# Thirty small transfers of a two-block fp32 kernel asked for by ScalarE's queue instead of SyncE's

## The chip, the cores and the metric

The kernel runs on one core of a Trainium2 chip. The metric is the device time of one execution in microseconds; the median of three runs of the kernel before is 1255.97 us. PE is the matrix engine, ACT is ScalarE, DVE is VectorE, POOL is GpSimd and SP is SyncE. SP does no arithmetic here: its queue only asks for transfers (DMAs). ACT can ask for transfers too, from the same instruction stream in which its activations stand.

## The reference, cut to what matters

Input x is 256 tokens by 1024 channels in fp32. A first block mixes with a gated delta rule and a banded attention and ends in a gated MLP; a second block of two layers puts 16 meta tokens ahead (272 rows) and mixes with a gated linear attention and a forgetting attention. The change touches three places of it: the cumulative decays `g` of the delta rule, the triangular solve of the delta rule, and the cumulative forget gates `c` of the forgetting attention.

```python
def chunk_gated_delta_rule(q, k, v, g, beta):        # block 1, 8 heads, chunks of 64
    g = jnp.cumsum(g, axis=-1)
    diff = g[..., :, None] - g[..., None, :]
    decay = jnp.where(causal, jnp.exp(jnp.where(causal, diff, 0.0)), 0.0)
    a_low = jnp.where(strict, jnp.einsum("bnhid,bnhjd->bnhij", k_beta, k) * decay, 0.0)
    rhs = jnp.concatenate([v_beta, k_beta * jnp.exp(g)[..., None]], axis=-1)
    sol = lax.linalg.triangular_solve(a_low + eye, rhs, left_side=True, lower=True, unit_diagonal=True)
    ...                                              # scan over the chunks with u, w = split(sol)

def forgetting_attention(q, k, v, log_f):            # block 2, both layers, 8 heads
    c = jnp.cumsum(log_f.astype(jnp.float32), axis=1)
    logits = jnp.einsum('bqhd,bkhd->bhqk', q_b, kf) + c_b[..., None] - c_k[:, :, None, :]
    logits = jnp.where(key_pos[None, :] <= q_pos[:, None], logits, -jnp.inf)
    return jnp.einsum('bhqk,bkhd->bqhd', jax.nn.softmax(logits, axis=-1), vf)
```

## The kernel before, in words

**Weights.** All weights lie in one array `wall` and are read once, in the order in which they are used, in pieces of mostly 1 MB (`load`, L341) into three buffers `raw`. Each piece holds two tiles of 128x1024. For full fp32 accuracy a tile is split in a high and a low part: ACT copies it to `wh` (four buffers, L313), DVE takes the rest into `wl` (four buffers, L316), and PE multiplies three times (`xh` by `wh`, `xl` by `wh`, `xh` by `wl`, L328): 24 matmuls of 256 or 272 columns per tile. So ACT and DVE must each finish a tile before PE comes to it, and a `raw` buffer is free for SP's next request when both are done with its tiles. L313, L316, L325, L328 and L332 are helpers: nearly every ACT, DVE and PE instruction has one of these lines.

**The places that the change touches.** In `delta_setup` DVE scans the decays into `g`; L827 writes them to a DRAM scratch `gd`. In `decay`, for a pair of heads at a time, L880 reads two rows of `gd` back, repeated over all 128 partitions (its tile is called `k` in the trace). In `delta_rest` L923 writes the diagonal parts of the scores to a scratch `ld` (two transfers), L927 reads the 16x16 diagonal blocks back (`td`), DVE inverts the blocks in 15 steps (L936), L944 writes the inverses and their transposes to `ed0` and `ed1`, and L946 reads both back as full matrices `ee`, which the delta rule's matmuls then use. In block 2, once in each layer, L1419 writes the scanned forget gates to a scratch `cd`, and eight transfers (L1425 and L1426, for four pairs of heads) read them back repeated over 128 partitions as `X2` (272 KB each) and `X1` (144 KB each). ACT meanwhile computes `dec` and `ge` for the linear attention. DVE copies `X0` from `X1` (L1444), POOL masks them (L1446), DVE subtracts scores and takes the maximum (L1503, `fp`), ACT exponentiates, DVE normalises (`fpp`), and PE transposes `fpp` (L332).

**What sets the order.** The program is written as generators, but the order of the instructions on each engine is made by `_Order`: a list scheduler with a table of durations, which goes through time, starts on each engine the ready instruction of highest priority, and then fixes that order. In the kernel before, all transfers are on SP; their model has one chain of 440 ns per request (`ring`) and one of transfer times (`wire`), 1200 ns (`SLACK`) are added to the end of each transfer that isn't a weight or an input, and such a transfer may run at most 24 PE instructions ahead of its place in the program.

**Completion.** A transfer counts up one of eight completion semaphores, named DMAHW0 to DMAHW7 in the listings below, which are handed out in turn over all transfers; a transfer may therefore have to wait until an older one with the same semaphore has landed.

## Time and profile before

| what | value |
|---|---|
| median of three runs | 1255.97 us (1250.74, 1258.10, 1255.97) |
| the profiled execution's own time | 1249.03 us |
| its span, first to last instruction | 1247.3 us |
| mean granted clock of PE | 0.995 |
| busy share: PE, DVE, ACT, POOL | 98%, 82%, 63%, 2% |
| moved by DMA | 232.59 MB, mean 186 GB/s |

The profile is of one execution. A timeline gives an instruction's start and duration; "idle before" is the time for which its engine had nothing to do, with the work that ended it. The chain that ended last goes back from the last instruction over what released each. The duration of a transfer's line on SP is the time that the request took on the queue; when the data is there is told as "to landing". The profiled execution is 6.9 us under the median of the three runs, 0.5%.

### The profile page before, as it was taken

Reading aid. Unit: us, or ns where it says so; the run is one execution under the profiler, and the core shown is the slowest. Engines: PE = TensorE matmul, PEld = TensorE weight load, DVE = VectorE, ACT = ScalarE, POOL = GpSimd, SP = SyncE. Lnnn points to the kernel's source line nnn. Section 1 sums busy time; section 2 is a strip of 40 time slices with the busy share of each in tenths; the row PEclk is TensorE's granted clock in tenths of the full one; section 3 lists DMA queues with packets and bytes.
Section 4 is the critical chain, followed back from the end, with each engine's and each line's share of the span. In section 5 each row is a group of like instructions: output and inputs, shape, how many; then the busy total and the mean of one; then the engine's idle time right before and its main releaser. Section 6 shows DMA issues by size and latency. Waiting matters only on the chain.

```text
span 1247.3 us, 24659 instructions
## 1 busy us (share of the span) xinstructions
PE 1219.5 (98%) x9824; PEld 1166.4 (94%) x9824; DVE 1017.8 (82%) x2098; ACT 781.8 (63%) x1451; POOL 22.2 (2%) x79
## 2 busy tenths in 40 slices
PE   7999999999999899999999999999999999999997
PEld 6898999989999899999877999999999979999996
DVE  6767898789999999767967989996567688999854
ACT  5577855346657768546766776665466576766642
POOL 0000100000000000000020000000001000000000
PEclk9999999999999999999999999999999999999998
DMA  9945577717663576554341444555455326555551
GB/s 360 368 170 188 203 256 234 300 35 265 213 231 137 178 274 220 187 189 169 116 177 69 164 174 171 170 168 183 164 179 192 116 69 203 188 184 181 180 186 47
DMA packets 51123, 232.59 MB, mean 186 GB/s; under 512 B 10536, under 2 KB 19904, under 8 KB 27456
## 3 DMA queue, kind: packets, MB, share of 16 engines
q1 hardware_dynamic: 51008, 231.02, 52.5%
q8 instruction: 77, 1.26, 0.4%
q14 instruction: 38, 0.31, 0.1%
HBM read 226.52 MB, written 4.48 MB: 185 GB/s over the span
## 4 chain that ended last, share of the span: by engine, by line
PE 84%; DVE 7%; DMA 4%; ACT 2%; issue 1%; SPq 0%; DVEq 0%; ACTq 0%
PE acc L328 60%; PE att L328 22%; DMA raw<-wall 3%; PE att L332 3%; DVE wl L316 2%; DVE raw L325 1%; DMA X<-cd 1%; ACT wh L313 1%; DVE res L316 0%; ACT tmp L313 0%; DVE fy L325 0%; DVE fp L1503 0%; DVE xl L316 0%; ACT L313 0%; ACT bq L313 0%
## 5 line engine op out<-in xcount | busy, mean ns | idle before, releaser
L313 ACT ACTIVATE wh<-raw 128x1024 fp32r<-128x1024 f32 (+1 forms) x367 | 381.5, 1042 | 280.8 <-PE acc L328 212.6
L316 DVE TENSOR_TENSOR wl<-raw,wh 128x1024 fp32r<-128x1024 f32 (+1 forms) x367 | 442.2, 1207 | 110.0 <-ACT wh L313 107.5
L328 PE MATMUL acc<-xh,wh 128*128 128x256 f32 (+2 forms) x1312 | 380.2, 291 | 1.4 <-ACT xh L313 0.9
L328 PE MATMUL acc<-xh,wl 128*128 128x256 f32 (+2 forms) x1312 | 374.9, 286 | 0.7 <-DVE wl L316 0.7
L328 PE MATMUL acc<-xl,wh 128*128 128x256 f32 (+2 forms) x1312 | 374.7, 286 | 0.0
L328 PEld LDWEIGHTS acc<-xh,wh 128*128 128x128 f32 x1312 | 246.7, 188 | 6.7 <-issue 2.4
L328 PEld LDWEIGHTS acc<-xh,wl 128*128 128x128 f32 x1312 | 247.4, 189 | 2.9 <-issue 1.4
L328 PEld LDWEIGHTS acc<-xl,wh 128*128 128x128 f32 x1312 | 247.4, 189 | 2.0 <-issue 1.5
L328 PE MATMUL att<-xh,wh 128*128 128x256 f32 (+2 forms) x568 | 161.2, 284 | 1.5 <-ACT wh L313 1.5
L328 PE MATMUL att<-xh,wl 128*128 128x256 f32 (+2 forms) x568 | 161.2, 284 | 0.4 <-DVE wl L316 0.4
L328 PE MATMUL att<-xl,wh 128*128 128x256 f32 (+2 forms) x568 | 161.1, 284 | 0.0
L328 PE MATMUL acc<-ah,wl 128*128 128x256 f32 (+1 forms) x528 | 149.9, 284 | 0.0
L328 PE MATMUL acc<-al,wh 128*128 128x256 f32 (+1 forms) x528 | 149.9, 284 | 0.0
L328 PE MATMUL acc<-ah,wh 128*128 128x256 f32 (+1 forms) x528 | 149.8, 284 | 0.0
L328 PEld LDWEIGHTS att<-xh,wh 128*128 128x128 f32 x568 | 106.8, 188 | 2.4 <-ACT wh L313 2.0
L328 PEld LDWEIGHTS att<-xh,wl 128*128 128x128 f32 x568 | 106.9, 188 | 0.7 <-DVE wl L316 0.6
L328 PEld LDWEIGHTS att<-xl,wh 128*128 128x128 f32 x568 | 106.8, 188 | 0.4
L328 PEld LDWEIGHTS acc<-al,wh 128*128 128x128 f32 x528 | 100.2, 190 | 0.0
L328 PEld LDWEIGHTS acc<-ah,wh 128*128 128x128 f32 x528 | 100.1, 190 | 0.0
L328 PEld LDWEIGHTS acc<-ah,wl 128*128 128x128 f32 x528 | 100.0, 189 | 0.0
L325 DVE SCALAR_TENSOR_TENSOR fy<-fsr,vec,fy 128x256 f32<-128x256 f32 (+2 forms) x176 | 85.6, 489 | 2.1
L325 DVE SCALAR_TENSOR_TENSOR raw<-raw,cact 128x1024 f32<-128x1024 f32 x48 | 58.6, 1221 | 18.3 <-DMA raw<-wall 13.6
(367 smaller groups left out, 1935.9 us busy)
## 6 DMA issues: line engine op xcount, KB each, us to landing
raw<-wall SPq DMA_DIRECT2D x183, 1024.0 KB, 4.9
raw<-wall SPq DMA_DIRECT2D x23, 896.0 KB, 4.5
X<-cd SPq DMA_DIRECT2D x8, 272.0 KB, 5.3
bq<-band SPq DMA_DIRECT2D x8, 256.0 KB, 6.1
ed<-td SPq DMA_DIRECT2D x2, 1024.0 KB, 11.3
X<-cd SPq DMA_DIRECT2D x8, 144.0 KB, 5.1
raw<-wall SPq DMA_DIRECT2D x2, 512.0 KB, 5.3
k<-gd SPq DMA_DIRECT2D x4, 256.0 KB, 5.5
```

What stands on the lines that cost most here:

```text
L313: return self.nc.scalar.activation(out=out, in_=in_, func=func, **k)
L316: self.nc.vector.tensor_tensor(out=out, in0=a, in1=b, op=op)
L325: self.nc.vector.scalar_tensor_tensor(out=out, in0=a, scalar=s, in1=b, op0=op0, op1=op1, **k)
L328: self.nc.tensor.matmul(out, lhsT, rhs, start=start, stop=stop)
L332: self.nc.tensor.transpose(out, in_, self.ident[p0:p0 + n, p0:p0 + n])
```

## The change

`self.small` names the queue of the small transfers. It was SP's and is now ACT's; L827, L880, L1419, L1425 and L1426, which named SP's queue directly, take `self.small` as well, and the four places of `delta_rest` (L923, L927, L944, L946) took it already, so they move with it. These are 12 transfers in block 1 and 9 in each layer of block 2, 30 in all. The rest of the diff is in the scheduler: the moved transfers keep their costs of the SP table, but have a chain `side` of their own beside the weights', get 600 ns added to their end instead of the 100 ns and the `SLACK`, take 400 ns of ACT's time each, and the rule of 24 PE instructions no longer holds for them.

```diff
--- before.py
+++ after.py
@@ -260,7 +260,7 @@
         for idx, n in self.chunks:
             self.coff.append(o)
             o += n * P
-        self.small = self.nc.sync
+        self.small = self.nc.scalar
         self.raw, self.hl, self.pre = {}, {}, {}
         self.loaded = self.split = 0
         self.cur = 0
@@ -824,7 +824,7 @@
         self.ts(e, e, nega)
         nc.vector.tensor_tensor_scan(out=g, data0=self.c("rst", 0, S, 32, 40), data1=e, initial=0.0, op0=MUL, op1=ADD)
         gd = self.pd.tile([8, S], F32, tag="gd", name="gd")
-        nc.sync.dma_start(out=gd, in_=g)
+        self.small.dma_start(out=gd, in_=g)
         self.gd = gd
         G = [g[:, 64 * c + 63:64 * c + 64] for c in range(4)]
         br = self.t(pa, (40, 6, P), "ee")[R]
@@ -877,7 +877,7 @@
         b0 = self.bT[:, 0:32].rearrange("p (c h) -> p h c", h=8)[:, h:h + 2, :]
         b1 = self.bT[:, 32:48].rearrange("p (c h) -> p h c", h=8)[:, h:h + 2, :]
         grow = self.t(pa, (P, 2, S), "k2", 4)
-        nc.sync.dma_start(out=grow, in_=self.gd[h:h + 2].rearrange("h s -> (h s)").unsqueeze(0).to_broadcast([P, 2 * S]))
+        self.small.dma_start(out=grow, in_=self.gd[h:h + 2].rearrange("h s -> (h s)").unsqueeze(0).to_broadcast([P, 2 * S]))
         M = self.BQ[:, h:h + 2, 1, :]
         M0, M1 = M[:, :, 0:S], M[:, :, S:384]
         for j in range(2):
@@ -1416,14 +1416,14 @@
         nc.vector.tensor_tensor_scan(out=c, data0=self.c("ones", 0, 1, 32, 40).to_broadcast([8, L]), data1=E[R, 2, :],
                                      initial=0.0, op0=MUL, op1=ADD)
         cd = self.pd.tile([8, L], F32, tag=f"cd{i}", name=f"cd{i}")
-        nc.sync.dma_start(out=cd, in_=c)
+        self.small.dma_start(out=cd, in_=c)
         X2 = self.t(pa, (P, 8, L), "X2")
         X1 = self.t(pa, (P, 8, 144), "X1")
         X0 = self.t(pa, (NM, 8, NM), "X0")
         for m in range(4):
             h = slice(2 * m, 2 * m + 2)
-            nc.sync.dma_start(out=X2[:, h], in_=cd[h].rearrange("h s -> (h s)").unsqueeze(0).to_broadcast([P, 2 * L]))
-            nc.sync.dma_start(out=X1[:, h], in_=cd[h, 0:144].unsqueeze(0).to_broadcast([P, 2, 144]))
+            self.small.dma_start(out=X2[:, h], in_=cd[h].rearrange("h s -> (h s)").unsqueeze(0).to_broadcast([P, 2 * L]))
+            self.small.dma_start(out=X1[:, h], in_=cd[h, 0:144].unsqueeze(0).to_broadcast([P, 2, 144]))
         yield
 
         self.dec = dec = self.t(pa, (P, 2, 5), "dec")
@@ -1709,7 +1709,7 @@
             if i.is_transpose:
                 return max(2 * n, m) / 2.4 + 2
             return 4 * max(n, min(m, 128)) / 2.4 + (4 if int(ins[1].ap[0][1]) == 128 else 100)
-        if e == "SP":
+        if kind == "InstDMACopy":
             o = outs[0]
             rows = int(o.ap[0][1])
             dims = [(int(s), int(c)) for s, c in o.ap]
@@ -1829,7 +1829,8 @@
         for k in range(n):
             left[k] += len(self.deps[k])
             for j, after in self.deps[k].items():
-                succ[j].append((k, self.WAIT[eng[j]][E.index(eng[k])] if after or eng[j] != eng[k] else 0))
+                q = "SP" if self.ins[j].name in self.fix else eng[j]
+                succ[j].append((k, self.WAIT[q][E.index(eng[k])] if after or q != eng[k] else 0))
 
         prev = {}
 
@@ -1890,7 +1891,7 @@
                 heapq.heappush(soon[eng[k]], (0.0, k))
         for key in self.rows:
             give(key)
-        wire, ring, table, done = 0.0, 0.0, 0, 0
+        wire, side, ring, table, done = 0.0, 0.0, 0.0, 0, 0
         order = {e: [] for e in E}
         array = [0.0] * 8
         port = 0.0
@@ -1932,6 +1933,10 @@
                 if self.ins[k].name not in self.free:
 
                     end[k] += self.SLACK
+            elif self.ins[k].name in self.fix:
+
+                side = max(side, s + 440 + self.fix[self.ins[k].name]) + self.dur[k]
+                end[k], clock[e] = side + 600, s + 400
             elif len(self.cols.get(k, range(8))) < 8:
 
                 at = max([ready[k]] + [array[c] for c in self.cols[k]]) + self.dur[k]
```

The scheduler works out a new order for all engines; up to about 97 us of the run before it is the same. Three places of it matter below. In the listings names carry the buffers' numbers, and `waits` lists the semaphores that an instruction waits for.

**ACT at the end of the triangular solve (block 1).** The four requests `ed` (write the inverses) and `ee` (read them back) stand on SP before, among the weights:

```order
L341 DMA raw_459_2868<-wall 128x2048 [waits DMAHW3_49,DMAHW0_49,DVE_49]
L944 DMA ed_1069<-k_322_1974 128x16x16 [waits DVE_49,Pool_49]
L944 DMA ed_1070<-k_322_1974 128x16x16 [waits DVE_49]
L341 DMA raw_463_2901<-wall 128x2048 [waits DMAHW1_49,DVE_49]
L946 DMA ee_2099<-ed_1069 128x16x128 [waits DMAHW4_49]
L341 DMA raw_478_2987<-wall 128x2048 [waits DMAHW2_49,DVE_49]
L946 DMA ee_2099<-ed_1070 128x16x128 [waits DMAHW5_49]
L341 DMA raw_485_3029<-wall 128x2048 [waits DMAHW3_49,DVE_49]
```

and after the change on ACT, among the splits of the weight tiles:

```order
L944 DMA ed_1069<-k_322_1974 128x16x16 [waits DVE_49]
L313 ACTIVATE tmp_435_2712<-tmp_433_2705 128x256 [waits DVE_49,Activation_49]
L944 DMA ed_1070<-k_322_1974 128x16x16 [waits DVE_49]
L313 ACTIVATE wh_454_2832<-raw_443_2758 128x1024 [waits PE_49]
L313 ACTIVATE wh_460_2870<-raw_447_2791 128x1024 [waits DMAHW2_49,PE_49]
L946 DMA ee_2099<-ed_1069 128x16x128 [waits DMAHW4_49]
L313 ACTIVATE vb_1173<-acc_446_2789 128x256 [waits PE_49]
L313 ACTIVATE tmp_450_2821<-vb_1173,vec_67 128x256 [waits Activation_49]
L946 DMA ee_2099<-ed_1070 128x16x128 [waits DMAHW5_49]
L313 ACTIVATE wh_464_2903<-raw_459_2868 128x1024 [waits DMAHW3_49,PE_49]
L313 ACTIVATE tmp_456_2860<-acc_453_2831,hb_1635 128x256 [waits PE_49]
```

The second `ee` is ahead of the split `wh_464`, and waits for the landing of the second `ed` (DMAHW5) before anything behind it can start. On PE the first matmul that reads `ee` stood in row 1,532 of its order and now stands in row 1,487, 45 rows of single dense matmuls earlier.

**ACT at the gates of layer 0 (block 2).** Before, SP had `cd` and the eight `X` in one run, with the next weights behind:

```order
L341 DMA raw_1314_7997<-wall 128x2048 [waits DMAHW6_49,DVE_49,Activation_49]
L1419 DMA cd_7536<-gy_7511 8x272 [waits DVE_49,Pool_49]
L1425 DMA X_1228_7538<-cd_7536 128x544 [waits DMAHW2_49]
L1426 DMA X_1229_7539<-cd_7536 128x2x144
...
L1426 DMA X_1229_7539<-cd_7536 128x2x144
L341 DMA raw_1331_8089<-wall 128x2048 [waits DMAHW3_49,DVE_49]
L341 DMA raw_1354_8199<-wall 128x2048 [waits DMAHW4_49,DVE_49]
```

Now ACT has them, `cd` ahead of a table load and the first `X` behind the `dec` and `ge` activations:

```order
L313 ACTIVATE wh_1315_7999<-raw_1296_7896 128x1024 [waits DMAHW0_49,PE_49]
L1419 DMA cd_7536<-gy_7511 8x272 [waits DVE_49]
L313 ACT_TABLE_LOAD
L313 ACTIVATE dec_7551<-gy_7511 128x4 [waits DVE_49]
L313 ACTIVATE ge_7512<-ge_7512 128x272 [waits DVE_49]
L313 ACTIVATE dec_7551<-gy_7511 128x4
L313 ACTIVATE ge_7512<-ge_7512 128x272 [waits DVE_49]
L1425 DMA X_1228_7538<-cd_7536 128x544 [waits DMAHW2_49]
L1426 DMA X_1229_7539<-cd_7536 128x2x144
...
L1426 DMA X_1229_7539<-cd_7536 128x2x144 [waits DMAHW3_49]
L313 ACTIVATE wh_1323_8042<-raw_1296_7896 128x1024 [waits PE_49]
L313 ACTIVATE wh_1332_8091<-raw_1314_7997 128x1024 [waits PE_49]
```

What stood on ACT directly behind the last `ge`, the split `wh_1323`, now stands behind all eight requests. On PE the first transpose of `fpp` stands four dense matmuls later in the weight tile it interrupts (after 20 of the tile's 24 instead of 16). In layer 1 the order on ACT has the same form: `cd`, table load, `dec`, `ge`, `dec`, `ge`, eight `X`, then the split; there the first transpose of `fpp` stands 8 dense matmuls earlier than before.

## Rows read from the trace of the kernel before

**Rows 1.** The page: busy time, share of the span and instructions of each engine, and the chain that ended last, by engine and by line.

```profile
PE 1219.5 (98%) x9824; PEld 1166.4 (94%) x9824; DVE 1017.8 (82%) x2098; ACT 781.8 (63%) x1451; POOL 22.2 (2%) x79
...
PE 84%; DVE 7%; DMA 4%; ACT 2%; issue 1%; SPq 0%; DVEq 0%; ACTq 0%
PE acc L328 60%; PE att L328 22%; DMA raw<-wall 3%; PE att L332 3%; DVE wl L316 2%; DVE raw L325 1%; DMA X<-cd 1%; ACT wh L313 1%; DVE res L316 0%; ACT tmp L313 0%; DVE fy L325 0%; DVE fp L1503 0%; DVE xl L316 0%; ACT L313 0%; ACT bq L313 0%
```

**Rows 2.** Stretches of the core. Columns: from:to and length in us, then busy us (instructions) of PE, PEld, DVE, ACT and POOL, the granted clock, the DMA engines' busy share, GB/s.

```profile
110.00:125.00 15.00, 14.85 (x101) 12.33 (x100) 14.06 (x58) 10.87 (x37) 0.00 (x0) 1.00 0.20 72
180.00:205.00 25.00, 25.00 (x213) 25.00 (x212) 23.85 (x56) 13.56 (x20) 0.00 (x0) 1.00 0.68 254
...
240.00:250.00 10.00, 9.31 (x103) 7.82 (x101) 8.53 (x19) 2.97 (x7) 0.00 (x0) 1.00 0.57 215
590.00:615.00 25.00, 23.73 (x156) 20.54 (x156) 23.42 (x61) 20.91 (x34) 0.55 (x6) 0.93 0.36 127
...
626.00:633.00 7.00, 5.84 (x47) 5.62 (x45) 5.14 (x24) 3.45 (x13) 5.03 (x12) 1.00 0.92 340
```

**Rows 3.** SP's queue at the end of the triangular solve. Two requests of weights from the timeline (start us, us, engine, line, operation, out<-in, count), then the lines L944 (`ed`) and L946 (`ee`): duration of a request in ns, shortest, median and longest, first and last start, and the time to landing.

```profile
211.86 1.91 SPq L341 DMA_DIRECT2D raw<-wall  x1
...
214.85 4.24 SPq L341 DMA_DIRECT2D raw<-wall  x1
...
L944 SPq DMA_DIRECT2D ed<-k x2: 377/2057/3737, 207.4 to 208.0; - x2
...
DMA to landing us min/median/max: 6.3/6.9/7.5
...
L946 SPq DMA_DIRECT2D ee<-ed x2: 691/738/785, 214.0 to 219.3; - x2
...
DMA to landing us min/median/max: 7.9/8.5/9.1
```

**Rows 4.** ACT over time in the same stretch; in brackets the idle time before the instruction and what ended it.

```profile
211.00 0.36 ACT L313 ACTIVATE vb<-acc 128x256 f32<-128x256 f32 x1
211.40 0.51 ACT L313 ACTIVATE tmp<-vb,vec 128x256 f32<-128x256 f32 x1
212.89 1.06 ACT L313 ACTIVATE wh<-raw 128x1024 fp32r<-128x1024 f32 x1 [0.98 <-PE acc L328]
```

**Rows 5.** The chain that ended last in 200 to 260 us (start us, us, what).

```profile
199.90 30.56 PE acc L328 x257
230.46 1.80 PE att L328 x16
```

**Rows 6.** SP's queue over time from 618 us on (`cd`, first and last `X` of layer 0), and two links of the chain that ended last there.

```profile
618.40 0.29 SPq L1419 DMA_DIRECT2D cd<-gy  x1
619.72 0.34 SPq L1425 DMA_DIRECT2D X<-cd  x1
...
623.38 0.43 SPq L1426 DMA_DIRECT2D X<-cd  x1
...
618.40 1.30 DMA cd<-gy
...
623.38 8.60 DMA X<-cd
```

**Rows 7.** ACT over time in the same stretch.

```profile
617.72 1.06 ACT L313 ACTIVATE wh<-raw 128x1024 fp32r<-128x1024 f32 x1 [0.57 <-PE acc L328]
618.80 1.28 ACT L313 ACT_TABLE_LOAD   x1
...
620.67 0.43 ACT L313 ACTIVATE ge<-ge 128x272 f32<-128x272 f32 x1
621.00 1.05 ACT L313 ACTIVATE wh<-raw 128x1024 fp32r<-128x1024 f32 x1
623.73 1.06 ACT L313 ACTIVATE wh<-raw 128x1024 fp32r<-128x1024 f32 x1 [1.68 <-PE acc L328]
```

**Rows 8.** DVE and PE over time from 631.5 us on.

```profile
632.01 0.17 DVE L1444 COPY X<-X 16x32 f32<-16x32 f32 x1 [1.86 <-DMA X<-cd]
...
631.55 0.29 PE L328 MATMUL acc<-xh,wh 128*128 128x272 f32 x1
633.11 0.63 PE L332 MATMUL att<-ident,fpp 128*128 128x128 f32 x3 [1.27 <-DVE fpp L320]
...
636.46 0.44 PE L332 MATMUL att<-ident,tl 128*128 128x128 f32 x2 [0.93 <-ACT ftA L313]
```

**Rows 9.** Layer 1, the same place: SP (last `X`), ACT and PE over time, and the time to landing of the `X1` transfers (line L1426, both layers).

```profile
941.41 0.50 SPq L1426 DMA_DIRECT2D X<-cd  x1
...
934.98 1.28 ACT L313 ACT_TABLE_LOAD   x1
937.30 0.21 ACT L313 ACTIVATE dec<-gy 128x4 f32<-128x4 f32 x1 [1.03 <-DVE gy L1433]
...
938.85 0.43 ACT L313 ACTIVATE ge<-ge 128x272 f32<-128x272 f32 x1
...
949.48 0.59 PE L332 MATMUL att<-ident,fpp 128*128 128x128 f32 x3
...
DMA to landing us min/median/max: 4.3/5.1/5.8
```

**Rows 10.** The line L880, the four transfers of decay rows: duration of a request in ns, shortest, median and longest, first and last start.

```profile
L880 SPq DMA_DIRECT2D k<-gd x4: 350/392/417, 137.3 to 143.7; - x4
```

## The prediction, made before the changed kernel was run

> **What bounds the kernel now.** I read the page first: PE is busy 98% of the span, 27.8 of 1247.3 us are left, and of the chain that ended last PE has 84%, DMA 4%, of which weights (`raw`) 3% and the read-back of the gates (`X<-cd`) 1% [rows 1]. So a faster transfer only pays where PE stands still for it. The table of stretches shows how little that is behind the start: 180 to 205 us runs 213 matmuls in 25 us without a gap, 0.1174 us each, and a 24-matmul tile takes 2.82 us [rows 2]. PE's stops are few: 0.69 us in 240 to 250 us, 1.16 us in 626 to 633 us, and a thin stretch at 590 to 615 us with 156 matmuls where 213 would fit, where no moved transfer stands [rows 2].
>
> Then I went to the three places of the change. The `ed` and `ee` transfers of block 1 end a chain that PE reaches at 230.46 us straight after 30.56 us of weights [rows 5]: it doesn't wait for them. In layer 0 PE does wait: the chain goes from `cd` over the last `X` (issued at 623.38, 8.60 us long) [rows 6] to DVE's copy at 632.01, which had waited 1.86 us for it, and to the transpose of `fpp` at 633.11, for which PE had stood idle; another 0.93 us of idle time stands before 636.46 [rows 8]. In layer 1 the transpose at 949.48 has no idle time noted before it [rows 9]. So the moved transfers cost PE some 1.4 us in layer 0 and nothing elsewhere. That, not the queues' business, is what can be won directly.
>
> **What the change costs, part by part.** Numbers are differences against the profiled execution (1249.03 us with 1247.3 us of span); I add them to the median of the runs, 1255.97 us, which lies 6.9 us above. A measurement of this kernel tells about 0.5%, 6.3 us, from no change.
>
> *Decay rows (gd, four grow).* ACT gets five requests of 0.35 to 0.42 us [rows 10], 2 us in all, and the first read-back waits on ACT until `gd` has landed; the nearest price for that is `cd`, 1.30 us [rows 6]. Queued behind it are ACT's bias and exponential activations. In 110 to 125 us ACT is busy 10.87 of 15 us and PE 14.85 of 15 [rows 2], so 4 us of room stand against at most 3.4. I take 0; bounds 0 and +1.3. SP loses five requests and weights could be asked for earlier, which is worth nothing while PE runs at 99%.
>
> *Diagonal blocks (ld, td, ed, ee).* Here ACT runs behind a wait. It issues `ed0` at about 207.4 and `ed1` at 208.0. On SP one of these two took 3.74 us, as did weight requests beside them, 1.91 and 4.24 us [rows 3]: the queue did not take them faster. `ee0` then waits for the landing of `ed0`, 6.3 us after 207.4, so 213.7, and takes 0.79; `vb` and `tmp` follow with 0.36 and 0.51 us [rows 4]; `ee1` waits for `ed1`, 208.0 + 7.5 = 215.5, issues at 215.7 and takes 0.69 by the rows of `ee`, or 4.24 by the slow weight beside it. Behind it is the split `wh_464`. Before, that split ran at 212.89, as soon as PE released its buffer [rows 4]; with four buffers three tiles stand ahead of it, 8.5 us, so PE needs it at 221.3. Now it runs at 216.4 to 219.9 and is finished, with 1.06 us, at 217.5 to 221.0: covered, barely in the worst case; without that cover each us of ACT is one of PE. The second thing queued is `ee` itself. PE's order takes its first matmul 45 dense matmuls earlier, 5.3 us, at 225.2 instead of 230.46. `ee1` issued at 215.7 lands after 7.9 to 9.1 us [rows 3], 223.6 to 224.8: in time. With the slow issue it is 229.0, and PE stands 3.8 us, with 0.9 more for DVE's half of the late split. I take 0 from the nearest rows (`ee`'s own); bounds −0.7 (the stop at 240 to 250 us goes, since SP asks for weights without `ed` and `ee` between them) and +4.7.
>
> *Gates of layer 0 (cd, eight X).* Before, SP issued `cd` at 618.40, the eight `X` from 619.72 to 623.81, 4.1 us in all [rows 6]. On ACT `cd` stands behind a split that ends at 618.78, and the eight behind the table load (1.28 us), two `dec` and two `ge`, which ended at 621.10 before [rows 7] and end about 621.4 with 0.29 us of `cd` ahead. So the `X` go out from 621.4 to 625.5, 1.7 us later, the last one starting at 625.1. The split behind them moves from 621.00 to 625.5; PE began that tile 16 matmuls before the transpose, about 629.7, and the split and DVE's `wl` take 2.3 us: covered. When the last `X` lands is open. If it takes 8.60 us again [rows 6] that is 633.7. If it has a weight of 1 MB more ahead, since SP is now free to ask for it 1.7 us sooner, add 2.8 us, 1.05 MB at 340 / 0.92 = 370 GB/s, the rate of the stretch from 626 us scaled to busy engines [rows 2]: 636.5. If it takes the median of these transfers, 5.1 us [rows 9], it is 630.2. From the landing to PE's transpose were 1.1 us (632.01 to 633.11). Without a stop PE would have come to the transpose at 631.67 (the matmul at 631.55 and one step), and comes 4 matmuls, 0.5 us, later by the new order: 632.17. So the stop is 633.7 + 1.1 − 632.2 = 2.6 us instead of 1.44. I take +1.2, by the landing of the same transfer; bounds −1.4 (630.2, no stop) and +4.0 (636.5).
>
> Here a rule speaks the other way. The Trainium skill (DMA: Bandwidth & Descriptors, section Queues, rings and completion order) says that SP and ACT each have rings of their own on the same 16 DMA engines, which take turns between them packet by packet. By that, `X` would not stand behind weights asked for earlier but share with them from its first request. By that rule `X` (1.66 MB) and as much of weights would take 9.0 us at 370 GB/s and, with the 1.3 us of `cd` as a start-up, be through at about 631.7; the stop would shrink to 0.6 us, and this term would be −0.8 instead of +1.2 (an estimate). No row of before shows two queues at work at once, so I keep 8.60 us for the sum.
>
> *Gates of layer 1.* The table load that ran at 934.98 in ACT's idle time before `dec` (1.03 us idle behind it) now stands behind `cd`, which waits for the scan at 936.6. `cd` to 936.9, table load to 938.2, `dec` and `ge` to 939.3, as late as before (938.85 + 0.43). The eight `X` go out from 939.3 on, the last starting at 942.8 instead of 941.41, 1.4 us later [rows 9]. Landing 5.8 us later (longest of the `X1`) is 948.6, and 1.1 us more to the transpose is 949.7. PE comes to it at 949.48 − 8 × 0.12 = 948.5: a stop of 1.2 us. Bounds: 4.6 us to landing hide it (0), 8.60 us give +4.0. I take +1.2.
>
> The sum is 0 + 0 + 1.2 + 1.2 = **+2.4 us, 1258.4 us**; the bounds add up to −2.1 and +14.0.
>
> **Rivals.** *ACT is held by its own requests (slower).* Issues on SP took 1.9 to 4.2 us where weights streamed [rows 3], against 0.3 to 0.5 in the quiet stretch before the `X` [rows 6]. If ACT's queue is held likewise, ACT stands with the splits behind it. It decides from about 3 us in one request: `ee1` then lands behind PE's earlier place (+3.8 to +4.7), and an `X` held for 2 us is late by 2 us more in both layers (+1.2 + 2 each). That is 4.2 + 3.2 + 3.2 = +10.6 us, 1266.6 us. For it: ACT now asks while SP asks too. Against: by rows 6 eight requests in a row were taken at 0.5 us each.
>
> *The queue helps (faster).* The moved transfers overtake weights, SP asks for weights earlier, and the named stops go: 1.4 in layer 0, 0.9 behind it, 0.7 at 240 to 250, −3.0 us, 1253.0 us. To go beyond 0.5% the new order must also fill part of the thin stretch at 590 to 615 us, where 57 matmuls, 6.7 us, are missing: −7, 1249 us. The rule of the Trainium skill above is on its side. Against: PE hardly waits for any of these transfers.
>
> *Hidden anyway (no change).* Both `X` land as early as before in the span that matters, 1256 us.
>
> **How the numbers follow.** The forecast of +2.4 us has a chance of 0.45, ACT held 0.27, the queue helps 0.18, hidden 0.10. Of the faster case I put two thirds, 0.12, beyond 0.5%, because there the whole order moves and the runs shown already differ by 7 us; of the slower case 0.24, and 0.02 of the forecast's upper bound, together 0.26. What is left, 0.62, is within 0.5%. The range goes from 1249.5 us (queue helps) to 1268 us (ACT held, and a little less than the upper bounds together).
>
> **What would show it.** Right: `X` issued on ACT about 621.4 to 625.5 with 0.3 to 0.8 us each, the last landing at 633 to 634, PE idle 2 to 3 us before the transpose of `fpp` in layer 0 and about 1 us in layer 1; `ee` landed before PE's first use. Wrong: requests of 2 us and more on ACT; idle time on PE before the first `ee` matmul or with ACT's `wh` as releaser near 220 us; `X` landing within 5 us of the request, so that the stop of layer 0 is gone; or a thin stretch at 590 to 615 us that has changed its number of matmuls.

## The result, and the profile after

The changed kernel takes 1270.89 us in the median of 4 executions (1263.97 to 1274.66), before 1257.03; the ratio is 1.0117 with a 95% interval of 1.0082 to 1.0152. In another 6 executions the ratio is 1.0130 (1.0080 to 1.0180). It is slower by about 15 us; the range ended at 1268.0. One execution each of ld_td_only (6628 us), of gd_only (2508 us) and of the kernel before (1269.5 us) lies far above the others of its kernel and is left out everywhere below.

The profiled execution took 1268.23 us, with a span of 1266.5 us (before 1247.3). The chain that ended last by engine, a line as in [rows 1]:

```profile
PE 77%; DVE 10%; DMA 6%; ACT 4%; issue 2%; ACTq 1%; POOL 0%; DVEq 0%; POOLq 0%; SPq 0%
```

PE has lost 7 points of the chain to DVE, DMA and ACT. Stretches of the changed kernel, columns as in [rows 2]:

```profile
180.00:185.00 5.00, 5.00 (x44) 5.00 (x43) 3.96 (x7) 2.30 (x3) 0.00 (x0) 1.00 1.01 332
185.00:190.00 5.00, 1.53 (x13) 1.32 (x12) 3.15 (x8) 1.96 (x4) 0.00 (x0) 0.99 0.45 170
190.00:195.00 5.00, 5.00 (x32) 5.00 (x31) 3.76 (x14) 1.42 (x2) 0.00 (x0) 0.67 0.75 259
230.00:235.00 5.00, 3.98 (x33) 3.64 (x32) 2.81 (x4) 0.23 (x2) 0.00 (x0) 1.00 1.04 424
235.00:240.00 5.00, 2.24 (x11) 2.17 (x11) 3.71 (x6) 1.19 (x2) 0.00 (x0) 0.77 0.77 318
640.00:645.00 5.00, 2.98 (x24) 2.75 (x22) 2.94 (x17) 2.62 (x13) 2.64 (x5) 1.00 0.82 278
645.00:650.00 5.00, 3.85 (x21) 3.01 (x21) 5.00 (x11) 2.85 (x5) 1.37 (x6) 0.73 0.33 107
...
690.00:695.00 5.00, 5.00 (x23) 3.44 (x25) 4.16 (x15) 1.55 (x6) 0.00 (x0) 0.50 0.01 3
695.00:700.00 5.00, 5.00 (x34) 3.52 (x32) 1.64 (x3) 1.81 (x5) 0.00 (x0) 0.50 0.00 0
```

At full pace there are 44 or 45 matmuls in 5 us of block 1 and 42 in block 2. PE stands still for 3.5 us at 185; in the 5 us behind it the granted clock, a mean over the stretch of its two levels 1.2 and 2.4 GHz, is 0.67. It stands for 1.0 and 2.8 us at 230 to 240, again with a lower clock behind it, and for 2.0 and 1.2 us at 640 to 650. At 690 to 700 it is busy all the time at a clock of 0.50, 1.2 GHz, with 57 matmuls in 10 us.

To see where the time goes, I compared both traces at equal amounts of PE work (the sum of the usual steps of all matmuls so far). The changed kernel is behind by 1.1 us at 180 us of the time of before, by 6.2 at 190, by 13.7 at 240, by 10.6 from 320 to 630 (it makes up about 3 us between 260 and 320), by 12.8 at 650, by 18.6 from 700 to 940 and by 19.2 at the end. So block 1's solve costs 9.5 us net, layer 0's gates 2.2, a stretch of low clock 5.8, layer 1's gates 0.6. In layer 0 the order on PE differs, so that the 2.2 and the 5.8 are parted only to about 1 us.

**The first stop.** The requests of `ld` and `td`, on SP before, and then ACT around them in the changed kernel, columns as in [rows 4]:

```profile
167.24 0.43 SPq L923 DMA_DIRECT2D ld<-bq  x1
...
174.45 0.38 SPq L927 DMA_DIRECT2D td<-ld  x1
```

```profile
170.59 0.48 ACT L313 ACTIVATE tmp<-acc,hb 128x256 f32<-128x256 f32 x1 [0.84 <-PE acc L328]
170.65 0.38 ACTq L923 DMA_DIRECT2D ld<-bq  x1
...
178.08 1.06 ACT L313 ACTIVATE wh<-raw 128x1024 fp32r<-128x1024 f32 x1 [1.05 <-DMA raw<-wall]
178.15 0.37 ACTq L927 DMA_DIRECT2D td<-ld  x1
```

The second `ld` stands behind an activation that waited for PE until 170.59 (in the kernel before SP asked for it at 167.24); its data had landed by 175.4, but `td` stands behind a split that waited for a weight until 178.08. It was asked for 3.7 us later than before (174.45), 2.8 us later when what the core was behind by then is taken off. DVE before, and in the changed kernel:

```profile
183.95 0.15 DVE L316 TENSOR_TENSOR td<-k,td 128x1 f32<-128x1 f32 x1
```

```profile
184.13 0.48 DVE L325 SCALAR_TENSOR_TENSOR tmp<-vb,vec,tmp 128x253 f32<-128x253 f32 x1
186.85 0.16 DVE L316 TENSOR_TENSOR td<-k,td 128x1 f32<-128x1 f32 x1 [2.23 <-DMA td<-ld]
```

`td` landed 8.7 us after the request (5.8 before). DVE waits 2.23 us for it, and the `tmp` that PE needs next is behind it on DVE (188.52); before, that `tmp` (179.35) stood ahead of it. PE's longest sums of waits, by what ended them (us in all, times, longest):

```profile
PE att L332 <- DVE fpp L320: 3.7, 3, 3.2
PE att L332 <- DVE tmp L325: 3.5, 1, 3.5
PE att L328 <- DVE k L316: 2.8, 1, 2.8
...
PE att L328 <- DMA ee<-ed: 1.0, 1, 1.0
...
PE acc L328 <- ACT wh L313: 0.5, 1, 0.5
```

The 3.5 us for `tmp` are the stop at 185; the 1.0 and the 2.8 are the stops at 230 to 240, the first for `ee`, the second for `k`; of 3.7 us for `fpp` 3.2 are in layer 0. For splits (`wh`) it waited 0.5 us directly, as before.

**The second stop**, ACT's requests with the time to landing of `ee` under them (to be held against [rows 3]):

```profile
212.89 3.90 ACTq L944 DMA_DIRECT2D ed<-k  x1
...
218.73 0.86 ACTq L946 DMA_DIRECT2D ee<-ed  x1
...
220.72 3.63 ACTq L946 DMA_DIRECT2D ee<-ed  x1
```

```profile
DMA to landing us min/median/max: 10.8/11.1/11.5
```

The second `ed` held ACT 3.90 us and the second `ee` 3.63. Both `ee` needed 10.8 to 11.5 us to land instead of 7.9 to 9.1, and the last landed at 232.3, 45 matmuls before its old place in PE's order: PE waited 1.0 us for it. The longer wait behind it, 2.8 us, was not for `ee`. The chain that ended last goes on from the held ACT:

```profile
224.46 1.07 ACT wh L313
...
228.25 1.15 DVE wl L316
...
229.42 5.33 DMA raw<-wall
...
234.85 1.07 ACT wh L313
...
235.95 1.23 DVE wl L316
237.17 0.61 DVE k L316
...
237.83 2.08 PE att L328 x8
```

The split behind the second `ee` was late, with it the low part `wl` on DVE, and so the buffer of that weight came free late (229.4); the next weight landed at 234.75, its split and its `wl` came behind it, and on DVE the `k` that PE waited for stood behind that `wl`. Before, two `k` stood ahead of the `wl`:

```profile
231.38 0.69 DVE L316 TENSOR_TENSOR k<-att,cst 128x512 f32<-128x512 f32 x1 [3.65 <-PE att L328]
...
232.89 1.22 DVE L316 TENSOR_TENSOR wl<-raw,wh 128x1024 fp32r<-128x1024 f32 x1
```

**Layer 0**: ACT's requests, the link of the chain that ended last, and DVE (compare [rows 6] and [rows 8]):

```profile
628.99 0.30 ACTq L1419 DMA_DIRECT2D cd<-gy  x1
...
631.31 0.37 ACTq L1425 DMA_DIRECT2D X<-cd  x1
...
636.12 0.48 ACTq L1426 DMA_DIRECT2D X<-cd  x1
```

```profile
632.71 9.33 DMA X<-cd
```

```profile
642.06 0.17 DVE L1444 COPY X<-X 16x32 f32<-16x32 f32 x1 [2.66 <-DMA X<-cd]
...
644.88 1.36 DVE L320 TENSOR_SCALAR fpp<-fp,den 128x272 f32<-128x272 f32 x3
```

Eight requests took 5.3 us. A weight was asked for on SP at 632.77, amid them; the `X1` issued at 632.71, the fourth request, took 9.33 us. In layer 1, where the next weight was asked for only at 963.9, after the last `X` (961.0), no `X` needed more than 5.7 us.

### The profile page after: what moved, and what is told of

Same layout as the page of the kernel before. It is cut to its first block, busy times and chain, and to the rows that moved or that the text cites. A ratio compares the mean times of both kernels' runs of the same rounds, so it can differ in the third digit from the quotient of the medians.

```text
span 1266.5 us, 24657 instructions
## 1 busy us (share of the span) xinstructions
PE 1229.9 (97%) x9824; PEld 1173.8 (93%) x9824; DVE 1019.4 (80%) x2098; ACT 783.8 (62%) x1453; POOL 24.6 (2%) x79
## 4 chain that ended last, share of the span: by engine, by line
PE 77%; DVE 10%; DMA 6%; ACT 4%; issue 2%; ACTq 1%; POOL 0%; DVEq 0%; POOLq 0%; SPq 0%
PE acc L328 52%; PE att L328 22%; DMA raw<-wall 3%; DVE wl L316 3%; PE att L332 3%; ACT wh L313 1%; DVE raw L325 1%; ACT L313 1%; DMA X<-cd 1%; DMA td<-ld 1%; DVE tmp L325 1%; DMA ed<-k 1%; DVE res L316 0%; ACT tmp L313 0%; DVE fp L1503 0%
## 5 line engine op out<-in xcount | busy, mean ns | idle before, releaser
L325 DVE SCALAR_TENSOR_TENSOR raw<-raw,cact 128x1024 f32<-128x1024 f32 x48 | 58.7, 1223 | 12.7 <-DMA raw<-wall 8.1
## 6 DMA issues: line engine op xcount, KB each, us to landing
ed<-td SPq DMA_DIRECT2D x2, 1024.0 KB, 11.5
```

The lines of the kernel that those rows point to most:

```text
L325: self.nc.vector.scalar_tensor_tensor(out=out, in0=a, scalar=s, in1=b, op0=op0, op1=op1, **k)
```

## The experiments

All ratios are to before's executions on the same chip (medians 1254.0 to 1256.1). They stand with their intervals as recorded and are not the quotients of the medians beside them; in runs of 4 executions the two differ by up to 0.4%.

| run | median us (executions) | ratio (95% interval) |
|---|---|---|
| b1_only | 1265.8 (10) | 1.0096 (1.0066 to 1.0126) |
| b2_only | 1257.5 (10) | 1.0007 (0.9975 to 1.0038) |
| ld_td_only | 1264.2 (9) | 1.0053 (1.0016 to 1.0089) |
| ed_ee_only | 1258.4 (10) | 1.0012 (0.9983 to 1.0042) |
| gd_only | 1256.4 (9) | 1.0015 (0.9990 to 1.0039) |
| ld_old_plan | 1253.4 (10) | 0.9990 (0.9959 to 1.0022) |
| ee_old_plan | 1254.2 (10) | 1.0000 (0.9967 to 1.0033) |
| delta_old_plan | 1254.3 (10) | 1.0001 (0.9969 to 1.0033) |
| sp_optplan | 1262.8 (10) | 1.0082 (1.0044 to 1.0121) |
| mixed_plan | 1263.0 (10) | 1.0075 (1.0043 to 1.0108) |
| b2_old_plan | 1274.5 (4) | 1.0106 (1.0023 to 1.0190) |
| pool_queue | 1274.7 (4) | 1.0184 (1.0121 to 1.0247) |
| plan_wire | 1278.4 (4) | 1.0195 (1.0139 to 1.0251) |
| plan_slack | 1286.7 (4) | 1.0295 (1.0227 to 1.0364) |

**Which transfers.** Parts of the change alone; the others name SP's queue again, as here for `ed` and `ee`:

```diff
-            q.dma_start(out=EE[:, w]...
+            nc.sync.dma_start(out=EE[:, w]...
```

> Only block 1's 12 transfers on ACT, cd and X back on SP. Theory (the late `td` and the held ACT in the triangular solve cost the time, the rest is the clock in block 2): PE stops near 185 us (about 3.5 us) and near 231 to 237 us (about 4 us) as in the changed kernel, net +9 us against before, 1266 us. Rival (block 2's X transfers cost most): 0 to +2 us. Rival (the clock at 50% around 690 us comes from the new order of block 2): if the order of block 2 is again that of before, the clock stays at 1.0 there.

> Only block 2's 18 transfers (cd, X) on ACT. Theory: one stop of 2 to 3.5 us before the transpose of fpp in layer 0 instead of 1.44, +1 to +2 us; and +7 us more (1264 to 1266 us) if PE's thin stretch about 55 us later again lets the clock fall to 0.5, which would show that this is the price of block 2's new order. Rival (the X transfers themselves cost the time by contention): the stop is 5 us and more in both layers.

> Only ld and td (three transfers, L923 and L927) on ACT. Theory: td is again requested 3 to 4 us later than before and lands 8 to 9 us after the request, DVE waits for it and PE stops about 3.5 us near 185 us; +4 to +6 us. `ee`, on SP, is asked for late by what the solve is late, and its place on PE is early, so a stop near 228 us is possible. Rival (only the held ACT at ed and ee costs): 0.

> Only ed and ee (four transfers, L944 and L946) on ACT. Theory: no stop near 185 us; ACT is held 3.9 us by the second ed and 3.6 us by the second ee, ee lands 11 us after its request instead of 8 to 9, PE stops at its first and second ee matmul, together 0 to 4 us since the solve is 5 us earlier than in the changed kernel. Rival (late td is the whole cause, the second stop only its echo): 0.

> Only gd and the four decay rows on ACT, with the new model. By the difference of b1_only (+10.6 us in the medians, +6.0 without the clock's part) and the two halves of the solve (+4.3 and +0.9 without the clock's part) it costs 0 to 2 us. If these five requests are what the two halves leave over in the medians, up to +4 us.

Block 1 carries nearly all, and in it `ld` and `td` the most. b1_only has stops of 3.2, 2.6 and 3.9 us for the same readers, ld_td_only one of 3.2 us at 184 us with DVE waiting 3.5 us for `td`, ed_ee_only 1.4 us for `ee` and 3.3 for `k`, part of which it gets back later. The expectation for gd_only and the order of the parts held. b2_only had the longer stop in layer 0 (4.2 us) but no measurable loss, and not the +7 us for the clock that its expectation allowed for.

**Queue or plan.** The change does two things: it puts transfers on another queue, and it lets the scheduler believe that they run on a lane of their own. These runs keep the queue and give the scheduler most of the old belief back, for `ed` and `ee`, for `ld` and `td`, and for all seven of the solve: the chain shared with the weights and the 1200 ns, though not the rule of 24 PE instructions and not the place in the chain of SP's requests.

```diff
-                side = max(side, s + 440 + self.fix[self.ins[k].name]) + self.dur[k]
-                end[k], clock[e] = side + 600, s + 400
+                wire = max(wire, s + 440 + self.fix[self.ins[k].name]) + self.dur[k]
+                end[k], clock[e] = wire + 100 + self.SLACK, s + 400
```

> Only ed and ee on ACT, and the scheduler models them on the weights' chain with the 1200 ns as before: the first ee matmul is back in row 1,532, PE's order differs from before in 10 lines. If the stop at ee (5 us in ed_ee_only) came from PE's place for ee, 45 matmuls early, there is none now, and the time is that of before within 2 us. If it came from the queue (ACT held, ee landing late), a stop of 3 us and more stays near 230 us.

> Only ld and td on ACT, with the old model for them. If the stop near 184 us comes from the plan, it is gone and the time is within 2 us of before. If it comes from the transfers themselves (the second ld and td land later because they share the DMA engines with the weights instead of standing ahead of them), td still lands 2 to 4 us later than before (180.2) and the stop is smaller, 0 to 2 us, by what the plan allows for.

> All seven transfers of the solve (ld, td, ed, ee) on ACT with the old model for them. PE's order differs from before in 129 lines. If the plan is the cause in block 1, the time is that of before within 3 us (the parts alone gave 0.999 and 1.000). If late td and late ee together are too much even for the old plan, +3 to +6 us.

No loss in any. Stretches of delta_old_plan (5.8 us behind before since 120 us, by a low clock there):

```profile
185.00:195.00 10.00, 10.00 (x86) 10.00 (x86) 9.68 (x24) 5.48 (x8) 0.00 (x0) 1.00 1.01 331
...
230.00:240.00 10.00, 10.00 (x88) 10.00 (x87) 2.87 (x4) 3.61 (x5) 0.00 (x0) 1.00 0.67 282
```

PE does not stop. What differs is told by `td`, in us, each run's times less what it was behind the kernel before at that place (good to some tenths):

| run | `td` asked for | landed | DVE comes to its first reader | DVE waits |
|---|---|---|---|---|
| before | 174.5 | 180.2 | 184.0 | 0 |
| changed kernel | 177.3 | 185.9 | 183.7 | 2.2 |
| ld_td_only | 175.5 | 182.5 | 179.0 | 3.5 |
| ld_old_plan | 177.5 | 183.0 | 183.9 | 0 |
| delta_old_plan | 176.7 | 183.0 | 183.9 | 0 |

The clean pair is ld_td_only and ld_old_plan: the same transfers on the same queue land within 0.5 us of each other, the reader stands 5 us earlier in one, and only there PE stops. DVE in ld_td_only and then in ld_old_plan:

```profile
184.12 0.16 DVE L316 TENSOR_TENSOR td<-k,td 128x1 f32<-128x1 f32 x1 [3.52 <-DMA td<-ld]
```

```profile
183.97 0.16 DVE L316 TENSOR_TENSOR td<-k,td 128x1 f32<-128x1 f32 x1
```

So it is for `ee`: in delta_old_plan the last one landed 4.0 us earlier against PE's work than in the kernel before, in ee_old_plan 0.4 us later, and in the changed kernel some 2 us earlier, where PE came to it 5 us earlier. In the changed kernel `td` is another matter. DVE comes to it when it did before, but it lands 5.7 us later: 2.8 by the later request, which is ACT's order, and 2.9 because it took longer to land. No run parts that longer landing from the order. What the runs show, then, is that ACT's queue alone, with these seven transfers on it, costs nothing in the solve, and that the order made under the new belief brings the stops, by the places of the requests as well as those of the readers.

A kernel with all transfers on SP and a more hopeful plan loses too:

```diff
-    SLACK = 1200
+    SLACK = 500
-            w = 24 if eng[k] == "SP" else None
+            w = None
```

> The kernel before, all transfers on SP, but with the optimistic plan: 500 ns instead of 1200 added, and no rule of 24 PE instructions. If the loss were the plan's optimism alone and not the queue, this loses too: +3 to +9 us. If it is ACT's queue: within 2 us of before.

It loses 8.1 us by the medians and 10 by the ratio, as this belief was expected to, or a little more. But it is not the belief of the change: the transfers still share the weights' chain, and the rule of 24 is dropped for all of SP's transfers. Most of the loss arises at 19 us, far from the solve, where PE waits 10.0 us in one piece for a weight asked for behind a request (L560) that held SP for 8.30 us and that the change does not move; near 250 and 320 us it loses some 3 and 2 us more. It says little on the solve.

**The old belief is no cure for the whole.** plan_wire has the diff with `wire` above for all 30 transfers, plan_slack only `side + 600 + self.SLACK`, b2_old_plan the diff with `wire` for block 2's transfers alone, mixed_plan the old belief for block 1's 12 and the new one for the rest (`B2` holds the names of block 2's):

```diff
+            elif self.ins[k].name in self.fix and self.ins[k].name not in B2:
+                ...
             elif self.ins[k].name in self.fix:
```

> The changed kernel with 1200 ns added again to the end of each moved transfer in the scheduler's model. Theory (the plan puts users of the transfers too early): the stops at td, ee and X shrink by about 1 us each, -2 to -5 us against the changed kernel, 1266 to 1269 us. Rival (the requests come late because ACT is in order, whatever the plan says): as the changed kernel, 1271 us.

> The changed kernel, but the scheduler's model lets the moved transfers and the weights share one chain of transfer times, as before, with the 1200 ns: the first ee matmul then stands 45 places later than before instead of 45 earlier. Theory: the stops at ee are gone (-4 us and its clock loss, -3), that at td partly; 1258 to 1264 us. Rival (requests late by ACT's order): stop at td as in the changed kernel, 1264 to 1271 us.

> Only block 2's cd and X on ACT with the old model for them. plan_wire lost 2% although the solve's halves lose nothing with the old model; the loss of its profile began at 640 us of the time of before, +3.3 at the X of layer 0, +6 at 680 and +10.6 at 690 us. If that is block 2's order, this loses 8 us and more; if it needs block 1's changes too, it is within 3 us of before.

> All 30 transfers on ACT as in the change; the old model (one chain with the weights, 1200 ns) for block 1's 12, the new one for block 2's 18. If the plan for block 1 is what the change pays for, the time is that of before or up to 4 us above (b2_only 1.0007, delta_old_plan 1.0001), against +15 us of the change. If ACT's queue itself costs, it stays at +8 us and more.

All lose. b2_old_plan is the first of its two cases; plan_slack and plan_wire missed; mixed_plan came out at the +9 us of its second case, that ACT's queue itself costs. In block 1 the stop at 185 us is gone in plan_wire and mixed_plan, but with the decay rows on ACT as well the last `ee` lands 15.4 and 15.6 us after its request, and some 6 to 7 us are lost between 230 and 300 us. In mixed_plan the chain that ended last runs through that landing itself: with these 12 transfers in this order the queue is not neutral, and what was found above holds for the seven alone. In block 2 the old belief itself does harm. ACT in b2_old_plan:

```profile
635.99 1.18 ACTq L1426 DMA_DIRECT2D X<-cd  x1
645.44 0.33 ACTq L1425 DMA_DIRECT2D X<-cd  x1
...
646.84 2.95 ACT L313 ACTIVATE wh<-raw 128x1024 fp32r<-128x1024 f32 x3 [11.84 <-DMA raw<-wall]
```

The seventh `X` was issued 8.3 us after the sixth ended, at the moment (645.42) at which the weight asked for at 635.0 landed, with whose completion semaphore it shares its own; three splits stood behind it, ahead of which ACT had computed nothing for 11.84 us, and PE stopped for 3.9 us.

**Another queue without anything behind it.** POOL is 2% busy:

```diff
-        self.small = self.nc.scalar
+        self.small = self.nc.gpsimd
```

> The 30 transfers on POOL's queue, which is 2% busy, instead of ACT's. If ACT's order (requests behind splits, splits behind requests) is the cause, the stops near 185 and 231 us go and the time is that of before or up to 3 us less. If two queues sharing the DMA engines are the cause (td and ee landing 3 us later than before), the stops stay: +4 to +10 us. POOL's own requests may take longer than ACT's; no run here shows that yet.

`td` was asked for at 172.64, right when `ld` had landed, and was there at 179.6. PE's largest waits:

```profile
PE att L332 <- DVE fpp L320: 10.2, 3, 6.3
PE att L328 <- DMA ee<-ed: 3.6, 1, 3.6
```

With +1.84% it lies outside both cases of its expectation. The stop at 185 us is gone, so there it was ACT's order that made `td` late for its reader. The others stay or grow: `ee` had been put 61 rows earlier and took 11.2 to 12.0 us to land, and the `X` of layer 0 landed up to 11.4 us after the request with two weights asked for amid them, a stop of 6.3 us.

**Two queues by themselves.** Transfers without the kernel. In the first try the sections ran into each other and tell nothing of sharing; the second orders them. The core of it:

```python
for name, q, wgt in (("sx", nc.sync, True), ("ax", nc.scalar, True), ("nx", nc.scalar, False), ...):
    for m in range(4):
        q.dma_start(out=big[:, h], in_=...)      # as X2
        q.dma_start(out=one[:, h], in_=...)      # as X1
    if wgt: nc.sync.dma_start(out=w, in_=...)    # 1 MB
```

> Not the kernel: only transfers. Twice over: eight X transfers with a weight of 1 MB behind them on SP (sx); the same with the X on ACT and the weight on SP asked for about 1 us later (ax); the X on ACT alone (nx); one ee-like transfer (2048 pieces of 512 B) with a weight behind it on SP (se), the same on two queues (ae), alone on ACT (ne). Theory (each DMA engine takes turns between the queues, and a turn of weights moves more bytes): in ax and ae the weight lands before or with the small transfer, and the last X and ee land 2 to 5 us later than alone; in sx and se the small transfers land as if alone, and the weight after them. Rival (a queue of its own puts small transfers ahead): ax and ae land like nx and ne.

> Only transfers again, now one section strictly after the other: sx, ax, nx, se, ae, ne twice over (X or ee-like on SP with a weight behind it, on ACT with the weight on SP about 1 us later, on ACT alone). Theory (shared DMA engines, turns between the queues): ae's transfer lands 2 to 5 us later than ne's and than se's, and its weight not later than itself; ax's last X lands 2 to 3 us later than nx's. Rival: ae like ne, ax like nx.

Time to landing of the `X1`-like transfers, alone on ACT, then on ACT with a weight on SP, then on SP with the weight behind them:

```profile
DMA to landing us min/median/max: 3.3/5.1/6.5
...
DMA to landing us min/median/max: 3.6/7.6/7.9
...
DMA to landing us min/median/max: 3.4/4.9/7.8
```

With a weight on the other queue the median of the `X1` is 7.6 us instead of 5.1; on one queue ahead of it they keep 4.9. The weight, asked for amid them, landed with the fourth. The rival is out for `X`. But a reader waits for the last of the eight, and that gains little by one queue: it landed 12.1 and 12.2 us after the first request with the weight on the other queue, 11.3 and 11.9 ahead of it on one, 9.4 and 10.7 alone. The `ee`-like transfer landed after 5.8 to 6.0 us alone, 6.1 to 7.1 with the weight on the other queue, 6.2 ahead of it on one: one weight a microsecond later doesn't explain the 10.4 to 12.7 us of `ee` on ACT in the kernels with the new belief (7.9 to 8.6 in delta_old_plan). What this does not rule out is the spacing: each `ee` is 1 MB like a weight. In the changed kernel the two were asked for 2.0 us apart with two weights just ahead of the second, 4 MB in all, for which the 424 GB/s of the row at 230 would need 9.9 us, by an estimate from that row; before, the two `ee` were 5.3 us apart. No run varies it.

**The spread.**

> The changed kernel again, in more executions, for the spread of the granted clock. If the time without the clock's part is the same in all executions and only the clock differs, then time and mean clock lie on one line as in the executions of before, and the changed kernel loses about 8 us in stops and 4 to 8 us by the clock.

The medians 1270.5 and 1270.9 agree. With the clock's part reckoned as span times what the mean clock lacks to 1, these 6 executions lie some 5 us above before without it (1248.1 to 1243.4), the first 4 some 8 (1251.9), and the rest of the 15 us is the clock. In its profile the solve costs 8.9 us, as in the first one, but the first stop only some 2 of it.

## Why the prediction was wrong

*What bounds the kernel.* Right: PE, and no gain was there to be had. No run was faster than before beyond its interval.

*Decay rows, 0 (to +1.3).* Profile +0.3 us; gd_only 1.0015 with no change inside the interval. Right within what can be told of them alone; in mixed_plan they stand with a loss that the seven others do not have by themselves.

*Diagonal blocks, 0 (−0.7 to +4.7).* **This step failed**: 9.5 us net in the profile, 8.9 in that of changed_again, 1.0096 in b1_only. First, I priced `ed` and `ee` and left `ld` and `td` without a price, though they stand in the same chain and ACT's order shows what they stand behind; with it `td` landed 5.7 us later, DVE, in order, waited 2.23 us for it, and PE lost 5.1 us (some 2 in changed_again). Second, I called the late split covered. It was, for its own tile; but it kept a weight's buffer, the next weight came late, and a `k` that PE needs stood behind that weight's `wl`: 2.8 us. Third, I took `ee`'s landing (7.9 to 9.1 us) from rows in which one queue kept the weights behind it, and it was 10.8 to 11.5, and I read PE's place for `ee`, 45 matmuls early, as a place that the transfer would just reach: 1.0 us. Behind all three is the order made under the scheduler's new belief: with the old one the same seven transfers on the same queue cost nothing (delta_old_plan, 1.0001). With the decay rows on ACT too they do cost under the old belief (mixed_plan, 1.0075); that part stays open.

*The clock* had no term. After each stop the granted clock was lower for a while: at 190 to 195 us PE was busy throughout and ran 32 matmuls instead of 45, some 1.5 us of the first 5.1; at 235 to 240 it was 0.77.

*Layer 0, +1.2 (−1.4 to +4.0).* The size was right: a stop predicted at 2.6 us was 3.2, and PE fell behind by 2.2 us (6.4 in changed_again with the low clock behind the stop). The `X` left between 631.3 and 636.6, which is 620.7 to 626.0 without the 10.6 us that the core was behind; predicted 621.4 to 625.5. The way to it is in part luck. The landing that decided was that of the fourth request after 9.33 us, 2.3 us earlier than the one predicted for the last, and from it to PE's transpose it took 4.1 us, not 1.1, since DVE had a weight's `wl` in between.

*The rule weighed there* would have made this −0.8. That queues take turns, as the Trainium skill has it (DMA: Bandwidth & Descriptors, section Queues, rings and completion order), agrees with two_queues_2, where the weight on the other queue brought the median of the `X1` from 5.1 to 7.6 us. My estimate from it had the wrong sign: the small transfers do not gain by the turns, the weight does, which would have stood behind them on one queue. The Trainium skill's sentence that asking from several engines only saves the time of asking (same page, section Issuing engines are not separate DMA queues) agrees with delta_old_plan, which gained nothing (1.0001, 0.9969 to 1.0033).

*Layer 1, +1.2 (0 to +4.0).* 0.6 us: the last `X` landed 5.4 us after its request.

*Rivals.* "ACT is held by its own requests" named the sign, +10.6 us and the condition, 3 us in one request, which was met twice (3.90, 3.63). Its mechanism does not make the first stop, the larger one; it makes the second by a longer way than the rival had, the late buffer instead of PE's wait for a split. "The queue helps" is refuted for every part. The chance of 0.26 for slower was too low, since it counted one of three things that could fail in the same chain.

**Open** is which interaction makes the solve late when the decay rows are on ACT with the old belief too (mixed_plan against delta_old_plan), and why `td` needs 8.7 us and `ee` 11 in the kernel; for the 5.8 us at 690 us see the last section.

## What to carry to other kernels

A transfer moved to a compute engine's queue stands behind everything that this engine waits for (`td` was asked for 2.8 us later here): go through every link of the chain, and ask of each what is in front of it and who, in order, stands behind its reader. Ask the same of the work behind the request: a split that came late by a request of 3.6 us kept a buffer, and PE stopped 2.8 us for what came of that. When a scheduler gets a new cost for a transfer, price the readers' new places before the transfers: with `td` landing as in ld_old_plan, a reader 5 us earlier gave ld_td_only a stop of 3.2 us. A queue of its own didn't put small transfers ahead of a large one here (7.6 us against 5.1 alone); one queue with the small ones first kept most of them there (4.9), but not the last.

## What the runs showed of the hardware

One kernel spreads by 16 us, and nearly all of it goes with the clock. 31 executions of the kernel before took 1248.45 to 1264.79 us, with mean granted clocks from 0.997 to 0.984; the correlation is −0.93. PE's order in b2_only is that of before up to 595 us. Before from 110 to 120 us, and then b2_only from 110 to 125:

```profile
110.00:115.00 5.00, 4.85 (x28) 3.56 (x27) 4.09 (x18) 2.08 (x5) 0.00 (x0) 1.00 0.15 26
115.00:120.00 5.00, 5.00 (x37) 4.19 (x36) 4.96 (x21) 4.51 (x13) 0.00 (x0) 1.00 0.46 188
```

```profile
110.00:115.00 5.00, 4.85 (x23) 3.53 (x22) 4.13 (x17) 2.08 (x5) 0.00 (x0) 0.84 0.19 34
115.00:120.00 5.00, 5.00 (x21) 3.66 (x21) 2.45 (x8) 2.73 (x6) 0.00 (x0) 0.50 0.43 180
120.00:125.00 5.00, 5.00 (x21) 4.37 (x20) 5.00 (x25) 2.77 (x13) 0.00 (x0) 0.50 0.00 0
```

The first 5 us have the same busy time on PE, 4.85 us, with waits between thin matmuls; in one execution the clock stayed at 2.4 GHz, in the other it fell to 1.2 within them and stayed there for over 10 us, 5.3 us lost. So a low clock that one profile shows behind thin work is not the change's by that alone. The changed kernel's 5.8 us at 690 us are such a case: in the profile of changed_again the clock is 1.00 there, and low at 110 to 125 (5.7 us) and behind the stop of layer 0 (0.50 at 655). PE's order from 640 to 720 us is the same in b2_only as in the changed kernel, and there too the clock at 690 is 1.00; b1_only has the order of before in that stretch, in which the clock before was 1.00, and fell to 0.50 at 690. What is the change's: 10 executions of the changed kernel had mean clocks of 0.975 to 0.989, and its stops are further places at which the clock can fall.

A request on ACT waited 8.3 us for a weight on SP's queue to land, with which it shares its completion semaphore (b2_old_plan): two queues are not independent where the program hands both the same semaphores.
